# One step of a gated linear recurrence: where the value products of a 128-row block are written

## The chip, the core and the metric

The kernel runs on one core of a Trainium2 chip. TensorE (PE in the profile) multiplies matrices into PSUM banks, VectorE (DVE) and ScalarE (ACT) read those banks and round or combine, GpSimd (POOL) works on data in SBUF, and SyncE (SP) issues most of the DMAs. Each engine works through its own list of instructions in order; the engines wait for each other by semaphores. The metric is the device time of one execution in microseconds. A run's time is a little longer than the span in its profile, which goes from the first to the last instruction.

## The reference

One layer of a hybrid decoder runs on a prompt of 1024 rows and on 64 rows of 8 sampled sequences, with model width 1024. Both go through a gated feed-forward part (FFN, inner width 2816), a mixer and a second FFN. The mixer projects its input once, and splits the result between sliding-window attention and a gated linear recurrence with four heads of 128 keys and 128 values. The recurrence in the reference, cut to what matters:

```python
def step(S, inp):
    qb, kb, gb, vb = inp
    G = jnp.cumsum(gb, axis=2)
    ...
    A = jnp.einsum('bhtk,bhsk,bhtsk->bhts', qb, kb, decay)
    o = jnp.einsum('bhts,bhsv->bhtv', A, vb) + jnp.einsum('bhtk,bhkv->bhtv', qb * jnp.exp(G), S)
    G_last = G[:, :, -1:, :]
    S = jnp.exp(G_last[:, :, 0, :])[..., None] * S + jnp.einsum(
        'bhsk,bhsv->bhkv', kb * jnp.exp(G_last - G), vb)
    return S, o
...
o = rms_norm(o, hg_out_norm[l]) * jax.nn.silu(hg...)
```

For each chunk of rows there is an output `o`, made from the masked products `A` with the values and from the queries with the old state `S`, and a new state, made from the decayed old one and from keys times values. The output is then normalised per head and multiplied with a gate.

## The kernel before

**Tiling.** The rows are cut into three parts: part 0 has 320 (256 of the prompt and the 64 sampled ones), parts 1 and 2 have 384 each. The recurrence goes in blocks of 128 rows: two in part 0, three in each of the others, eight in all. Every large product is made of three products of rounded halves (`mm3`, L258 to L262), with the weights as `hi` and `lo`: the cast L240 on ACT, the difference L241 on DVE. These are the rows named `mm` in the profile.

**Two kinds of work interleaved.** The large products are written out in order: projections of the first FFN, `w_in` of a part, `w_out` of a part, and so on. The mixer of a part is a Python generator that runs beside them. After every few products the code calls `tick()`, and a tick advances each running stream by its rate (0.88, 1.08 and 1.24 steps for the mixers of parts 0, 1, 2); a step is what a generator does up to its next `yield`. Beside the mixer, streams for the norms run in the same way. Part 0's mixer runs beside the last products of the first FFN, part 1's beside `w_out` of part 0 and `w_in` of part 2, part 2's beside `w_out` of part 1 and the first columns of the second FFN. `need(...)` runs what is left of a stream to its end.

**Inside the mixer.** `mixer(n)` takes steps in turns from two chains (`both`): the recurrence (`intra`, then one `hgrn_block` per block) and the attention (`attn_block` per block, in part 0 also the sampled rows). `intra` builds the masked products `At` and the decayed queries `Q` and keys `K` of the whole part. A `hgrn_block` then goes in these steps:

- keys: four transposes `kT` (L1446) into a PSUM bank, copied to `kn` by ACT (L1448). In the first block of a part one empty step follows (L1450 to L1451).
- values: `av`, the products of `At` with the values (L1454) and, except in the very first block, of `Q` with the state `st` (L1457).
- state: `u`, the products of `kn` with the values (L1461), then the update of `st` by DVE (L1463 or L1466). In the same step `finish_hgrn` begins: squares of `av` by ACT (L1400), the mean (L1401) and the root (`rsqrt`, L212 to L229) on DVE, and the scaling of `av` by it (L1403).
- two empty steps, then the transposes `hT` (L1409), the gate (L1411) and the rounding into the input of `w_out` (`put_mix`, L1196 and L1197).

**Buffers.** PSUM has eight banks: four for the large products (tag `mm`) and four (tag `ax`) that `kT`, `av`, `u`, `hT`, the attention's `sc`, `pT`, `pv`, `pvT`, `oT`, the transposes `tr` and the means `rb` share. `av` holds its bank from its first product to L1403, `u` to the update of the state.

**Order.** The kernel's context has a planner: `TileContext(nc, schedule_with_timeline_sim=True)`. It takes the order in which the code is written as priority and makes each engine's list with timings of its own model; an instruction that its model holds not ready lets later ones pass. So the written place of an instruction is a priority and not a position: in the trace the squares L1400 stand ahead of `u` in several blocks, though they are written behind it. Where buffers of a tag are all taken, an instruction that needs one waits in that plan.

Of the kernel before, what the change touches and what calls it, by code (L numbers as in the profile page):

```python
# [47 lines left out]
def tile_step(ctx: ExitStack, tc: tile.TileContext, A: dict, O: list):  # L48
# [17 lines left out]
    def axbank(s="ax"):  # L66
        return ps.tile([P, 512], F32, tag="ax", bufs=4, name=uid(s))
# [1011 lines left out]
    def mixing(tp, h):  # L1079
        w_in, w_out = A["w_in"], A["w_out"][0]  # L1080

        def t2(shape=(P, 512)):
            return tmp2("t2", shape)
# [311 lines left out]
        def finish_hgrn(n, bank, r, c0):  # L1395
            sm = small()
            o = t2((P, 4, P))
            b4 = bank.rearrange("p (a t) -> p a t", a=4)
            for a in range(4):
                S.activation(o[:r, a], b4[:r, a], AF.Square, accum_out=sm[:r, 0, a:a + 1])  # L1400
            V.tensor_scalar(sm[:r, 0, :4], sm[:r, 0, :4], 1.0 / P, EPS, op0=ALU.mult, op1=ALU.add)  # L1401
            rsqrt(sm[:r, 1, :4], sm[:r, 0, :4], (sm[:r, 2, :4], sm[:r, 3, :4]))
            V.tensor_tensor(o[:r], b4[:r], sm[:r, 1, :4].unsqueeze(2).to_broadcast([r, 4, P]), op=ALU.mult)  # L1403
            yield
            yield
            yield
            tb = axbank("hT").rearrange("p (a t) -> p a t", a=4)
            for a in range(4):
                PE.transpose(tb[:, a, :r], o[:r, a], ident[:r, :r])  # L1409
            m = t2((P, 4, P))  # L1410
            V.tensor_tensor(m[:, :, :r], tb[:, :, :r], Z[n]["g"][:, :, c0:c0 + r], op=ALU.mult)  # L1411
            put_mix(n, 1, slice(c0, c0 + r), m[:, :, :r])
            yield
# [21 lines left out]
        def hgrn_block(n, b):  # L1435
            z = Z[n]
            c0 = b * P
            first = state[0] is None
            if first:
                state[0] = tp.tile([P, 4, P], F32, tag="st", name="st")  # L1440
            st = state[0]
            At, Q, K, D = [M[n][i] for i in ("At", "Q", "K", "D")]
            cs = slice(c0, c0 + P)
            tb = axbank("kT").rearrange("p (a t) -> p a t", a=4)
            for a in range(4):
                PE.transpose(tb[:, a], K[:, a, cs], ident)  # L1446
            kn = t2((P, 4, P))
            S.copy(kn, tb)  # L1448
            yield
            if b == 0:  # L1450
                yield  # L1451
            ob = axbank("av")
            for a in range(4):
                PE.matmul(ob[:, a * P:(a + 1) * P], At[:, b, a], z["v"][:, b, a * P:(a + 1) * P],  # L1454
                          start=True, stop=first)
                if not first:
                    PE.matmul(ob[:, a * P:(a + 1) * P], Q[:, a, cs], st[:, a], start=False, stop=True)  # L1457
            yield
            ub = axbank("u").rearrange("p (a t) -> p a t", a=4)
            for a in range(4):  # L1460
                PE.matmul(ub[:, a], kn[:, a], z["v"][:, b, a * P:(a + 1) * P], start=True, stop=True)  # L1461
            if first:
                V.tensor_copy(st, ub)  # L1463
            else:
                for a in range(4):
                    V.scalar_tensor_tensor(st[:, a], st[:, a], D[:, a, b:b + 1], ub[:, a],  # L1466
                                           op0=ALU.mult, op1=ALU.add)
            yield from finish_hgrn(n, ob, P, c0)
# [156 lines left out]
        def mixer(n):  # L1625
            MT[n] = new_h(n)
            at = [attn_block(n, b) for b in range(NPB[n])]
            M[n] = {}
            hg = [intra(n, M[n])] + [hgrn_block(n, b) for b in range(NPB[n])]
            if n == 0:  # L1630
                at = at + [sample_attn(), kv_out(0)]
                hg = hg + [sample_hgrn()]
            if n == 2:
                at.append(kv_out(2))
            yield from both(chain(*hg), chain(*at))
            if n == 2:
                nc.sync.dma_start(O[4][0, 0].rearrange("h k v -> k h v"), state[0])
# [277 lines left out]
```

## Time and profile before

| what | value |
|---|---|
| median of 3 runs | 1936.35 us (1936.21 to 1937.49) |
| profiled execution, its own time | 1939.13 us |
| its span, first to last instruction | 1937.4 us |
| TensorE busy | 1923.1 us, 99% of the span |
| VectorE, ScalarE, GpSimd busy | 1430.7, 946.0 and 186.1 us |
| granted TensorE clock, mean | 0.999 |
| DMA | 375.56 MB, mean 194 GB/s |

A row of a timeline has the start in us from the span's start, the length in us, the engine, the line of the code, the operation, the tiles written and read, the shape, and how many instructions of that kind follow each other; in brackets stands how long the engine was idle before it, and who ended that. Matmuls are pipelined, so the next one starts before the last one's row ends: the distance of two starts is what a matmul takes of TensorE's time. One of these products in 32-bit floats goes as two instructions, so four products of 128 columns are "x8". A row of the waits has who waited, for whom, the sum in us, the number of times and the longest. The mixers of the three parts lie between about 690 and 1320 us.

### The profile page before, as it was taken

What the parts mean: (1) busy time and instruction counts of PE and PEld (TensorE: products, weight loads), DVE (VectorE), ACT (ScalarE), POOL (GpSimd) and SP (SyncE); (2) the same over time, 40 slices, a digit from 0 to 9 for tenths busy, and PEclk for the clock granted to TensorE, in tenths of its full rate; (3) what the DMA queues carried; (4) which work ended last, traced back from release to release, by engine and by line L of the source; (5) the groups of instructions that cost most, each with busy time, mean ns of one, the idle gap of its engine ahead of it and who ended that gap; (6) DMA issues with size and microseconds to landing.
All of it is one profiled execution on the core that took longest, in us unless ns stands there. A gap on an engine that the chain in (4) does not pass through costs nothing.

```text
span 1937.4 us, 34843 instructions
## 1 busy us (share of the span) xinstructions
PE 1923.1 (99%) x13547; PEld 1806.1 (93%) x13547; DVE 1430.7 (74%) x2469; ACT 946.0 (49%) x1701; POOL 186.1 (10%) x227
## 2 busy tenths in 40 slices
PE   9999999999999999999999999999999999999998
PEld 9999999999998987788999888989999999999886
DVE  6896789877568666787678758756987887656666
ACT  5553444444455434545445545846544444445452
POOL 0300000000004022020221212000000000000102
PEclk9999999999999999999999999999999999999999
DMA  6643676555767556765334344546555555667974
GB/s 248 209 133 115 232 267 247 206 191 184 242 217 242 180 155 215 283 220 163 114 102 153 99 140 142 164 147 209 185 198 192 198 188 189 210 228 241 308 255 141
DMA packets 175750, 375.56 MB, mean 194 GB/s; under 512 B 16144, under 2 KB 67536, under 8 KB 175568
## 3 DMA queue, kind: packets, MB, share of 16 engines
q1 hardware_dynamic: 169680, 362.84, 56.0%
q10 hardware_dynamic: 5904, 10.49, 1.5%
q8 instruction: 106, 1.74, 0.4%
q14 instruction: 60, 0.49, 0.1%
HBM read 290.86 MB, written 83.39 MB: 193 GB/s over the span
## 4 chain that ended last, share of the span: by engine, by line
PE 88%; DMA 6%; DVE 3%; ACT 1%; issue 1%; POOL 1%; SPq 0%; ACTq 0%; DVEq 0%; POOLq 0%
PE mm L260 27%; PE mm L262 26%; PE mm L261 26%; DMA ar<-fa 1%; DMA xt<-in_x_rest_dram 1%; DMA ar<-act 1%; PE lv L1337 1%; PE sc L1237 1%; DMA raw<-in_ffn_w_gu_dram 1%; PE pv L1283 1%; DVE w L241 1%; PE pT L1269 1%; PE c L262 0%; PE c L260 0%; PE c L261 0%
## 5 line engine op out<-in xcount | busy, mean ns | idle before, releaser
L260 PE MATMUL mm<-h,wsph 128*128 128x320 f32 (+1 forms) x1344 | 427.2, 319 | 0.4 <-DVE big L814 0.4
L261 PE MATMUL mm<-h,wsph 128*128 128x320 f32 (+1 forms) x1344 | 425.5, 317 | 0.2 <-DVE h L241 0.2
L262 PE MATMUL mm<-h,wspl 128*128 128x320 f32 (+1 forms) x1344 | 422.6, 316 | 0.0
L241 DVE TENSOR_TENSOR wspl<-raw,wsph 128x1024 fp32r<-128x1024 f32 x208 | 260.8, 1255 | 125.2 <-ACT wsph L240 124.1
L240 ACT CAST wsph<-raw 128x1024 fp32r<-128x1024 f32 x208 | 217.8, 1049 | 254.0 <-PE mm L261 199.3
L260 PEld LDWEIGHTS mm<-h,wsph 128*128 128x128 f32 x1344 | 252.2, 188 | 4.2 <-issue 2.3
L261 PEld LDWEIGHTS mm<-h,wsph 128*128 128x128 f32 x1344 | 252.5, 188 | 3.9 <-issue 2.3
L262 PEld LDWEIGHTS mm<-h,wspl 128*128 128x128 f32 x1344 | 251.9, 188 | 3.4 <-issue 3.1
L240 ACT CAST w<-raw 128x512 fp32r<-128x512 f32 (+1 forms) x208 | 153.8, 745 | 199.9 <-PE mm L261 96.2
L261 PE MATMUL mm<-h,w 128*128 128x384 f32 (+1 forms) x736 | 245.6, 334 | 0.3 <-DVE h L622 0.3
L260 PE MATMUL mm<-h,w 128*128 128x384 f32 (+1 forms) x736 | 245.7, 334 | 0.2 <-ACT h L620 0.2
L262 PE MATMUL mm<-h,w 128*128 128x384 f32 (+1 forms) x736 | 239.6, 333 | 0.5 <-POOL w L613 0.4
L241 DVE TENSOR_TENSOR w<-raw,w 128x512 fp32r<-128x512 f32 (+1 forms) x208 | 178.3, 861 | 72.6 <-ACT w L240 71.7
L261 PE MATMUL mm<-w,h 128*128 128x512 f32 x462 | 180.5, 391 | 0.7 <-DVE w L241 0.7
L260 PE MATMUL mm<-w,h 128*128 128x512 f32 x462 | 180.8, 394 | 0.0
L262 PE MATMUL mm<-w,h 128*128 128x512 f32 x462 | 179.8, 391 | 0.0
L260 PE MATMUL mm<-big,w 128*128 128x384 f32 x528 | 176.7, 335 | 0.3 <-ACT big L806 0.2
L261 PE MATMUL mm<-big,w 128*128 128x384 f32 x528 | 176.5, 334 | 0.0
L262 PE MATMUL mm<-big,w 128*128 128x384 f32 x528 | 176.0, 334 | 0.0
L261 PEld LDWEIGHTS mm<-h,w 128*128 128x128 f32 x736 | 138.1, 188 | 1.1 <-DVE h L622 0.8
L260 PEld LDWEIGHTS mm<-h,w 128*128 128x128 f32 x736 | 138.1, 188 | 0.8 <-ACT h L620 0.5
L262 PEld LDWEIGHTS mm<-h,w 128*128 128x128 f32 x736 | 137.6, 188 | 1.0 <-POOL w L613 0.7
(367 smaller groups left out, 3353.8 us busy)
## 6 DMA issues: line engine op xcount, KB each, us to landing
raw<-in_ffn_w_gu_dram SPq DMA_DIRECT2D x162, 512.0 KB
raw<-in_ffn_w_down_dram SPq DMA_DIRECT2D x74, 512.0 KB
raw<-in_w_in_dram SPq DMA_DIRECT2D x54, 512.0 KB
ar<-fa SPq DMA_DIRECT2D x70, 384.0 KB
big<-in_ffn_w_down_dram SPq DMA_DIRECT2D x88, 256.0 KB
fb<-big SPq DMA_DIRECT2D x44, 512.0 KB
fa<-big SPq DMA_DIRECT2D x22, 768.0 KB
raw<-fb SPq DMA_DIRECT2D x30, 512.0 KB
```

The lines of the kernel that those rows point to most:

```text
L240: made['S'] = S.copy(hi, src).ins
L241: (lo_eng or V).tensor_tensor(lo, src, hi.bitcast(F32), op=ALU.subtract)
L260: PE.matmul(out, a[0], b[0], start=first, stop=False, skip_group_check=resume)
L261: PE.matmul(out, a[0], b[1], start=False, stop=False, skip_group_check=resume)
L262: return PE.matmul(out, a[1], b[0], start=False, stop=last, skip_group_check=resume).ins
L1237: PE.matmul(banks[g][rows(hq), i, cs], zq[rows(g), 2 * pr + i, b * P + 64 * hq:b * P + 64 * hq + 64], kx[rows(g), k0 + cs.start:k0 + cs.st ...
L1269: PE.transpose(tb2[hq][:, g, i, slot], pt[g][rows(hq), c:c + P], ident[rows(hq), rows(hq)])
L1283: PE.matmul(ob[par][rows(g), :, hq], vn[rows(par), b + (blk + hq) // 2, rows(g)], pT[hq][rows(par), g, :, PLACE[hq][blk]], start=alone or ...
L1337: PE.matmul(b5[32 * i:32 * i + 32, b, a], K[:, a, cs], Q[:, a, cs], start=True, stop=True)
```

## The change

In `hgrn_block` the `yield` between the value products and the state products goes, and a `yield` is added behind the copy of the keys. The number of steps of a block is the same. The keys are transposed and copied in one step as before; then there is an empty step (two in a part's first block); then `av` and `u` are written in one step, `av` first, and `finish_hgrn` begins in it as before.

```diff
             kn = t2((P, 4, P))
             S.copy(kn, tb)
             yield
+            yield
             if b == 0:
                 yield
             ob = axbank("av")
...
                           start=True, stop=first)
                 if not first:
                     PE.matmul(ob[:, a * P:(a + 1) * P], Q[:, a, cs], st[:, a], start=False, stop=True)
-            yield
             ub = axbank("u").rearrange("p (a t) -> p a t", a=4)
             for a in range(4):
                 PE.matmul(ub[:, a], kn[:, a], z["v"][:, b, a * P:(a + 1) * P], start=True, stop=True)
```

## The prediction

> **What bounds the kernel.** I read the page's busy times first, then the stretches of the span, then TensorE's own waits, and last the timelines around the eight recurrence blocks.
>
> ```profile
> span 1937.4 us, 34843 instructions
> PE 1923.1 (99%) x13547; PEld 1806.1 (93%) x13547; DVE 1430.7 (74%) x2469; ACT 946.0 (49%) x1701; POOL 186.1 (10%) x227
> 690.00:960.00 270.00, 267.39 (x2328) 227.51 (x2327) 193.32 (x405) 125.27 (x249) 55.57 (x61) 1.00 0.60 193
> 960.00:1150.00 190.00, 190.00 (x1981) 175.67 (x1980) 139.69 (x282) 95.93 (x200) 41.88 (x60) 1.00 0.41 127
> 1150.00:1320.00 170.00, 169.27 (x1672) 151.63 (x1671) 116.19 (x255) 103.39 (x220) 18.52 (x32) 1.00 0.47 148
> ```
>
> The last three rows are the stretches of the mixer: length, then busy time of PE, PEld, DVE, ACT and POOL, then the granted clock. The reader is to see that TensorE hardly ever stands: 2.6, 0.0 and 0.7 us in the three. What stands there is listed whole in its waits between 690 and 1320 us:
>
> ```profile
> PE spT L1517 <- ACT t L1512: 1.3, 1, 1.3
> PE av L1454 <- ACT t L1292: 1.1, 1, 1.1
> PE pv L1283 <- DVE t L1274: 0.5, 2, 0.4
> PE kT L1446 <- POOL big L1388: 0.4, 1, 0.4
> ```
>
> So 1.3 + 1.1 + 0.5 + 0.4 = 3.3 us is all that better order could win back in the mixer. A loss has no such lid: whatever makes TensorE wait is added to the time.
>
> **The change part by part.** It removes no instruction, adds none, and issues no DMA elsewhere; nothing passes a DMA of SP's queue or work of POOL's. In each block the value products `av` (L1454, L1457) are written one step later, right ahead of the state products `u` (L1461). The number of steps stays, so `u`, the state update and all attention steps keep their places.
>
> First: how many blocks does that reach? In four of the eight, `av` and `u` already run back to back, because `av` had to wait: the second block of part 0 (its `av` is the wait of 1.1 us above) and the three of part 2. Here is the last of part 2, on TensorE:
>
> ```profile
> 1243.30 0.38 PE L1454 MATMUL av<-big,big 128*128 128x128 f32 x2
> 1245.08 1.06 PE L1461 MATMUL u<-big,t 128*128 128x128 f32 x8
> 1189.09 1.06 PE L1461 MATMUL u<-big,t 128*128 128x128 f32 x8
> 1189.91 0.39 PE L260 MATMUL mm<-h,wsph 128*128 128x320 f32 x1
> 1190.14 0.31 PE L261 MATMUL mm<-h,wsph 128*128 128x320 f32 x1
> 1190.28 0.31 PE L262 MATMUL mm<-h,wspl 128*128 128x320 f32 x1
> ```
>
> `av` takes 1245.08 - 1243.30 = 1.78 us when `u` follows; `u` takes 0.82 (from the first block of part 2, third and fourth row), and the first projection behind it is 0.23 long where 0.14 is usual, 0.09 for the change of shape. Together 2.69 us. In the other four (the first block of part 0, all of part 1) projections lie between. The first `u` of part 1, and its second block:
>
> ```profile
> 1004.35 1.05 PE L1461 MATMUL u<-big,t 128*128 128x128 f32 x8
> 1029.82 0.38 PE L1454 MATMUL av<-big,big 128*128 128x128 f32 x2
> 1031.38 0.39 PE L1457 MATMUL av<-st,big 128*128 128x128 f32 x2
> 1031.52 0.42 PE L260 MATMUL mm<-h,wsph 128*128 128x384 f32 x1
> 1031.78 0.34 PE L261 MATMUL mm<-h,wsph 128*128 128x384 f32 x1
> 1035.76 1.05 PE L1461 MATMUL u<-big,t 128*128 128x128 f32 x8
> 1036.57 0.42 PE L260 MATMUL mm<-h,wsph 128*128 128x384 f32 x1
> 1036.83 0.34 PE L261 MATMUL mm<-h,wsph 128*128 128x384 f32 x1
> 1037.00 0.34 PE L262 MATMUL mm<-h,wspl 128*128 128x384 f32 x1
> ```
>
> Apart, `av` costs 1031.52 - 1029.82 = 1.70, `u` 0.81, and each is followed by a projection of 0.26 where 0.17 is usual: 1.70 + 0.81 + 2 x 0.09 = 2.69 us. Joined or apart is the same 2.69. Term for TensorE: 4 x 0.0 = 0.0 us.
>
> Second: what follows `av`. The squares on ACT (L1400), nine small steps (L1401 and the eight of the root) and the scaling L1403 on DVE, then the transposes `hT` (L1409) on TensorE. Counts and sizes stay; they are now due 6 us later, and the question is whether `hT` then finds its input. The tightest is the third block of part 1; its rows on ACT, DVE and TensorE:
>
> ```profile
> 1060.78 0.39 PE L1457 MATMUL av<-st,big 128*128 128x128 f32 x2
> 1061.20 0.28 ACT L1400 ACTIVATE t<-av 128x128 f32<-128x128 f32 x1 [0.54 <-PE av L1457]
> 1065.16 1.05 PE L1461 MATMUL u<-big,t 128*128 128x128 f32 x8
> 1066.30 1.28 ACT L1157 ACT_TABLE_LOAD   x1
> 1067.59 1.49 ACT L1157 ACTIVATE big<-big 128x1536 f32<-128x1536 f32 x1
> 1068.99 1.16 ACT L240 CAST h<-ht 128x320 fp32r<-128x320 f32 x3
> 1070.19 0.60 PE L1211 MATMUL oT<-ident,t 128*128 128x128 f32 x4
> 1072.97 0.69 DVE L1403 TENSOR_TENSOR t<-av,sm 128x512 f32<-128x512 f32 x1
> 1074.71 0.68 DVE L1197 TENSOR_TENSOR h<-oT,h 128x512 fp32r<-128x512 f32 x1
> 1074.83 0.89 PE L1237 MATMUL sc<-kx,big 64*64 64x192 f32 x16
> 1079.86 0.60 PE L1409 MATMUL hT<-ident,t 128*128 128x128 f32 x4
> ```
>
> `av` ended at 1060.78 + 0.39 = 1061.17 and L1403 started 11.8 us behind that. Put `av` where `u` starts, 1065.16; with 1.78 + 0.17 of its tail it ends at 1067.11, L1403 by the same distance starts at 1078.91 and ends at 1079.60, 0.26 us ahead of `hT`. No wait, but only just. The same sum in the block quoted above it: `av` ends 1037.71 in place of 1031.77, its L1403 and `hT` are
>
> ```profile
> 1037.24 0.69 DVE L1403 TENSOR_TENSOR t<-av,sm 128x512 f32<-128x512 f32 x1
> 1048.98 0.60 PE L1409 MATMUL hT<-ident,t 128*128 128x128 f32 x4
> ```
>
> and L1403 would end at 1037.24 + 5.94 + 0.69 = 1043.87, 5.1 us early. So for this term I take 0.0 us. Upper end, at the third block: ACT works in order, and the squares may come to stand behind the table load, the sigmoid and the casts, which end at 1070.15 in place of 1067.11. That is 3.04 us more; L1403 ends at 1082.64 and `hT` waits 2.78 us. I take the lower value, for the kept distance of 11.8 us is already the longest seen (5.5 us in the block before), so it holds DVE work that need not follow the squares.
>
> [...]
>
> Third: `u` now starts 1.78 us later, the update L1466 with it. The next reader of the state is the following block's `av`, no sooner than 1029.82 against the first `u` of part 1 at 1004.35: covered by over 20 us, 0.0.
>
> Fourth: PSUM. `av`, `u`, `oT`, `sc` and the mean of the norms share four banks. At 1074.83 `sc` needs two: `u`'s was free, and `av`'s came free at 1073.66, behind L1403. With L1403 late it takes `oT`'s, free at 1074.71 + 0.68 = 1075.39, 0.56 us later than now. Between 0 and 0.6; I take 0.0, since the planner has projections to put ahead of `sc`, and without these it costs the 0.6.
>
> Fifth: the wait of 1.1 us at `av` in part 0. Its block keeps its order, so 0.0; lower end -1.1.
>
> Sum: 0.0 + 0.0 + 0.0 + 0.0 + 0.0 on the profiled execution's 1939.13 us (span 1937.4 and 1.7 around it). The median of the runs shown is 1936.35, 2.8 us below that execution; the forecast against it is 1936.3.
>
> **The rivals.** (a) The later `av` of part 0 no longer meets the copy L1292: its 1.1 us go, 1935.2. For it: one step later, the copy is 1.1 us nearer its end. Against it: this `av` already runs behind its written place. If every wait of the mixer went, it would be 3.3 us, 1933.0.
>
> (b) `hT` is late in the third block of part 1: 1936.35 + 2.78 = 1939.1. For it: a margin of 0.26 us only. Against it: TensorE has projections at hand that the planner can put first.
>
> (c) Slower: vector and scalar work for the weights is held up behind the moved chain, in all three blocks of part 1. DVE and ACT take their work in order. If the planner places L1401 where it would have come on its own count and `av` is 5.94 us later, DVE stands up to that long, and the rounding of the next weights (L241) behind it. The cover is the weights that are ready ahead:
>
> ```profile
> ACT wsph L240 <- PE mm L261: 34.7, 19, 4.0
> ```
>
> In 960 to 1150 us the casts waited 19 times, up to 4.0 us, for TensorE to give a buffer back, so weights are about one tile of 24 products ahead, 24 x 0.17 = 4.1 us. From a stand of 4.1 us on it decides; at 5.94 us each block pays 1.8, three 5.5 us: 1941.9. Against it: the planner's order is made anew, with `av` in its new place, and in part 1 TensorE waited 0.0 us under the order that it made before.
>
> (d) The change does nothing: the planner draws `av` ahead again wherever TensorE has room. Same time as the forecast, 1936.3, but the rows of `av` would not move.
>
> **How the numbers follow.** No measurable change by the forecast 0.46, (d) 0.06, (a) 0.08, (b) 0.10: all within 0.2%, which is 3.9 us and about what a measurement of this kernel can tell from no change; together 0.70. (c) 0.24, slower by over 0.2%. Faster by over 0.2% needs more than the 3.3 us of waits in the mixer, so 0.06 for an order that also trims what I cannot see. The range goes down to 1933.0, all waits gone, and up to 1941.9, the whole of (c); beyond it I leave about 0.15. The likeliest case alone is 1935.2 to 1939.1.
>
> **What would show it.** In the trace after, each `u` of part 1 follows its `av` without a projection between, with 1.78 + 0.82 us; the four blocks that already ran so keep their order; TensorE stays at about 190.0 us busy of 190 in part 1; `hT` of the third block of part 1 waits under 1 us. (b) would show as a wait of `hT` for L1403, (c) as waits of projections for L241. The prediction is wrong if TensorE's waits in the mixer rise by 4 us or more, or if waits appear in stretches that the change doesn't touch, since the planner's order there was made anew as well.

## The result, and the profile after

The changed kernel takes 1942.53 us (median of 10 runs, 1941.56 to 1945.70) against 1937.82 us (median of 10, 1936.21 to 1939.19) of the kernel before, measured beside it: a ratio of 1.0026, with a 95% interval of 1.0018 to 1.0034. It is slower by 4.7 us, a little more than the 0.2% that a measurement can tell. I had forecast no change.

The top of the page after, and behind it the three stretches of the mixers (length, busy time of PE, PEld, DVE, ACT, POOL, clock, DMA):

```profile
span 1941.7 us, 34833 instructions
PE 1927.2 (99%) x13547; PEld 1808.4 (93%) x13547; DVE 1430.3 (74%) x2469; ACT 946.4 (49%) x1701; POOL 190.3 (10%) x227
```

```profile
690.00:960.00 270.00, 268.04 (x2331) 228.10 (x2331) 196.50 (x405) 125.55 (x250) 56.00 (x61) 1.00 0.60 193
960.00:1150.00 190.00, 190.00 (x1975) 174.84 (x1974) 138.53 (x280) 95.74 (x200) 42.64 (x60) 1.00 0.40 127
1150.00:1320.00 170.00, 168.79 (x1648) 149.40 (x1646) 113.80 (x246) 100.47 (x215) 19.45 (x32) 1.00 0.46 145
```

TensorE has the same 13547 instructions and the same clock, but is busy for 1927.2 us in place of 1923.1: the span grew by 4.3 us and the busy time by 4.1. In the mixers it stands 2.0 + 0.0 + 1.2 = 3.2 us, against 3.3 before. So in sum no wait was added. Of its waits in the mixers, that of `av` is 0.5 us shorter and that of `pv` 0.3 us longer; those of `spT`, 1.3, and `kT`, 0.4, are as before. The two that changed:

```profile
PE pv L1283 <- DVE t L1274: 0.8, 1, 0.8
PE av L1455 <- ACT t L1292: 0.6, 1, 0.6
```

Where does the busy time come from? The groups of TensorE's instructions between 690 and 1330 us show it, three groups of before and then the same three of after (count, busy time, mean ns of one, idle time before):

```profile
L1237 PE MATMUL sc<-kx,big 64*64 64x192 f32 (+1 forms) x256 | 15.6, 323 | 0.0
L1283 PE MATMUL pv<-t,vn 64*64 64x128 f32 x360 | 13.7, 278 | 0.5 <-DVE t L1274 0.5
L1269 PE MATMUL pT<-ident,t 64*128 64x64 f32 x240 | 12.8, 231 | 0.0
```

```profile
L1237 PE MATMUL sc<-kx,big 64*64 64x192 f32 (+1 forms) x256 | 16.5, 323 | 0.0
L1283 PE MATMUL pv<-t,vn 64*64 64x128 f32 x360 | 14.8, 279 | 0.8 <-DVE t L1274 0.8
L1269 PE MATMUL pT<-ident,t 64*128 64x64 f32 x240 | 14.0, 233 | 0.0
```

As many products, each as long as before (the mean of one is the same within 2 ns), and yet 0.9 + 1.1 + 1.2 = 3.2 us more of TensorE. These are the attention's three kinds of products on 64-row tiles (`64*64` and `64*128` where the projections have `128*128`), and the change touches none of them. By these sizes two or four such tiles fit where a projection takes 128*128, and products on different tiles ran at the same time: in the rows below, four of `sc` start within 0.1 us. Before, they did so more often. I call the products of one kind that follow each other on TensorE a visit. The third block of part 1 is the clearest place. Before, `sc` was one visit of 16 instructions, 1074.83 to 1075.65. After, on TensorE and DVE:

```profile
1074.80 0.87 PE L1237 MATMUL sc<-kx,big 64*64 64x192 f32 x8
1075.60 0.50 PE L260 MATMUL mm<-wsph,h 128*128 128x512 f32 x1
1075.93 0.40 PE L261 MATMUL mm<-wspl,h 128*128 128x512 f32 x1
1076.17 0.39 PE L262 MATMUL mm<-wsph,h 128*128 128x512 f32 x1
1077.41 0.87 PE L1237 MATMUL sc<-kx,big 64*64 64x192 f32 x8
1078.20 0.50 PE L261 MATMUL mm<-wspl,h 128*128 128x512 f32 x1
1075.53 0.68 DVE L1403 TENSOR_TENSOR t<-av,sm 128x512 f32<-128x512 f32 x1
```

Eight instructions take 1075.60 - 1074.80 = 0.80 us, and the other eight 0.79; all sixteen together took 0.82. `sc` writes two PSUM banks, and in the code each takes the products of one half of the array's rows (`banks[g]` those of `rows(g)`; `pT` and `pv` divide their banks likewise). How many of its instructions start within the first 0.1 us of the visit tells the two cases apart, before and then after:

```profile
1074.82:1074.92 0.10, 0.09 (x4) 0.09 (x8) 1.00 0.00 0
```

```profile
1074.79:1074.89 0.10, 0.09 (x2) 0.09 (x4) 1.00 0.00 0
```

Four at once with both banks, two at once with one. So a visit with one bank did half the work in the same time, 0.80 us against 0.82; I take the other half of the array to be empty then. (VectorE's L1247 reads two results at 1076.73 and 1077.00, ahead of the second visit at 1077.41, which fits one whole bank in each visit; the trace doesn't name the banks.) Why one bank: `av` now ends 4.1 us later (about 1065.3 in place of 1061.2), L1403 starts at 1075.53 in place of 1072.97, and L1197, which reads `oT`, stands behind it on DVE (at 1076.13 in place of 1074.71). At 1074.80 neither of their banks was free (L1403 ended at 1076.21, L1197 at 1076.81), and the planner put what it could, the half of `sc` whose bank was there. The price is 0.80 + 0.79 - 0.82 = 0.77 us, and 0.19 for one more change of shape there and back (1075.93 - 1075.60 = 0.33 where 0.24 follows, and some 0.1 on the product ahead): 1.0.

The second place is the second block of part 2, and there it is the transposes `pT` and the products `pv`. Before:

```profile
1228.83 1.01 PE L1269 MATMUL pT<-ident,t 64*128 64x64 f32 x16
1229.77 0.42 PE L260 MATMUL mm<-h,wsph 128*128 128x320 f32 x1
1232.49 0.90 PE L1283 MATMUL pv<-t,vn 64*64 64x128 f32 x24
1233.32 0.66 PE L1409 MATMUL hT<-ident,t 128*128 128x128 f32 x4
```

And after, with the row that follows each visit (a third single `pT`, 1229.25 to 1229.45, is left out):

```profile
1227.86 0.28 PE L1269 MATMUL pT<-ident,t 64*128 64x64 f32 x1
1228.07 0.41 PE L262 MATMUL mm<-h,wspl 128*128 128x320 f32 x1
1228.41 0.27 PE L1269 MATMUL pT<-ident,t 64*128 64x64 f32 x1
1228.61 0.42 PE L260 MATMUL mm<-h,wsph 128*128 128x320 f32 x1
...
1230.09 0.52 PE L1269 MATMUL pT<-ident,t 64*128 64x64 f32 x5
1230.54 0.42 PE L260 MATMUL mm<-h,wsph 128*128 128x320 f32 x1
1232.21 0.71 PE L1269 MATMUL pT<-ident,t 64*128 64x64 f32 x8
1232.85 0.55 PE L513 MATMUL tr<-ident,big 128*128 128x128 f32 x3
1233.90 0.65 PE L1283 MATMUL pv<-t,vn 64*64 64x128 f32 x8
1234.49 0.41 PE L262 MATMUL mm<-h,wspl 128*128 128x320 f32 x1
1235.72 0.87 PE L1283 MATMUL pv<-t,vn 64*64 64x128 f32 x16
1236.52 0.41 PE L260 MATMUL mm<-h,wsph 128*128 128x320 f32 x1
```

`pT` took 1229.77 - 1228.83 = 0.94 in one visit, and takes 0.21 + 0.20 + 0.20 + 0.45 + 0.64 = 1.70 in five. (Its 0.94 was not the best it can do: the visit of 16 at 961.73, shown with e14 below, takes 0.64. So in this block the kernel before had lost part of the overlap already.) `pv` took 0.83 and takes 0.59 + 0.80 = 1.39. That is 1.3 us, and five more changes of shape at 0.19 would be 1.0 (an estimate from the first place). In this block the change had swapped two things on ScalarE. The copy of the transposes `tr` (L518), which frees their PSUM bank, before and then after, beside the first exponential of the probabilities (L1255):

```profile
1225.03 0.46 ACT L1255 ACTIVATE t<-t,sm 128x192 f32<-128x192 f32 x1
1226.89 0.56 ACT L518 ACTIVATE big<-tr,cols 128x384 f32<-128x384 f32 x1
```

```profile
1224.56 0.58 ACT L518 ACTIVATE big<-tr,cols 128x384 f32<-128x384 f32 x1
1226.45 0.46 ACT L1255 ACTIVATE t<-t,sm 128x192 f32<-128x192 f32 x1
```

Before, `tr` and `av` lay between each other on TensorE, with three of `tr` even between `av` and `u`, and the copy came last. The end of it, before:

```profile
1224.33 0.39 PE L1457 MATMUL av<-st,big 128*128 128x128 f32 x2
1224.55 0.49 PE L513 MATMUL tr<-ident,big 128*128 128x128 f32 x3
1224.88 1.06 PE L1461 MATMUL u<-big,t 128*128 128x128 f32 x8
```

After, `av` is written later, `tr` goes first (its last before `av` at 1224.25), and its bank is free before the exponentials are done, which themselves begin 1.4 us later. My reading is that a bank for `pT` is there too soon, so that the plan places the transposes of this one bank singly, as it expects their inputs. The trace fits that in part: the first eight go one behind another and VectorE copies them at 1230.65, before the other eight begin at 1232.21. But the last exponential has ended at 1228.31, while the third single transpose goes at 1229.25 and the five at 1230.09, so it is the list that spaces them and not a wait. What the runs separate here is said with e6.

The third place is the third block of part 2, before and then after:

```profile
1273.66 0.89 PE L1283 MATMUL pv<-t,vn 64*64 64x128 f32 x24 [0.36 <-DVE t L1274]
```

```profile
1277.19 0.66 PE L1283 MATMUL pv<-t,vn 64*64 64x128 f32 x12 [0.85 <-DVE t L1274]
1277.78 0.44 PE L1301 MATMUL pvT<-ident,t 128*128 128x128 f32 x2
1278.15 0.65 PE L1283 MATMUL pv<-t,vn 64*64 64x128 f32 x12
```

Here `pv` is cut in two (0.59 and about as much again, in place of one visit of some 0.82) and its wait is 0.5 us longer. This cut is not one between the halves: four of the first twelve start within the first 0.1 us, as many as before, so both halves work in each visit, but each for a part of it alone.

To put a size on every place, the traces are aligned by work: from the distance of each two starts on TensorE the usual distance for that shape is taken, and what is left is added up. The difference to before in the three places (by the times of before), with the sum of the three groups above, for every run that follows:

```
run    1020-1080  1215-1245  1262-1300   sc+pv+pT, us    ratio [95%]
before     -          -          -         42.1            -
after    +1.4       +2.3       +0.9        45.3 (+3.2)   1.0026 [1.0018, 1.0034]
e1        0.0       +2.3       +0.9        44.2 (+2.1)   1.0015 [1.0006, 1.0023]
e2       +1.3        0.0        0.0        43.2 (+1.1)   1.0009 [1.0000, 1.0018]
e3       +1.4       +6.1       +0.9        43.9 (+1.8)   1.0034 [1.0021, 1.0047]
e4       +0.8       +6.4        0.0        41.7 (-0.4)   1.0021 [1.0012, 1.0029]
e5       +0.4       +2.3       +0.9        44.4 (+2.3)   1.0017 [1.0009, 1.0026]
e6        0.0       +0.5       +0.9        42.9 (+0.8)   1.0011 [1.0002, 1.0019]
e7       +0.3       -0.3        0.0        42.1 ( 0.0)   1.0003 [0.9994, 1.0012]
e8       +0.8        0.0        0.0        41.8 (-0.3)   0.9996 [0.9987, 1.0005]
e9       +0.3       +0.5       +0.9        43.2 (+1.1)   1.0006 [0.9998, 1.0015]
e10      +0.8       +2.3       -0.4        42.6 (+0.5)   1.0006 [0.9997, 1.0015]
e11      +0.3       +1.1       -0.4        41.2 (-0.9)   1.0000 [0.9991, 1.0009]
e12       0.0       +1.3       -0.8        40.6 (-1.5)   0.9995 [0.9986, 1.0004]
e13      +0.1       +0.5       -0.4        42.2 (+0.1)   0.9995 [0.9985, 1.0005]
e14      +0.5        0.0       +0.6        45.4 (+3.3)   1.0013 [1.0003, 1.0022]
```

For after, 1.4 + 2.3 + 0.9 = 4.6 us of the 4.7 measured. Ahead of 845 us, single profiled executions differ by up to 2.4 us, so a place is read more exactly than a whole span. For the kernels whose edits reach many blocks (e4, e8 and e10 to e14) the three places are not the whole: they also lose and gain elsewhere.

### The profile page after: what moved, and what is told of

Read it like the earlier page. It is cut to its first block, busy times and chain, and to the rows that moved or that the text cites. A ratio compares the mean times of both kernels' runs of the same rounds, so it can differ in the third digit from the quotient of the medians.

```text
span 1941.7 us, 34833 instructions
## 1 busy us (share of the span) xinstructions
PE 1927.2 (99%) x13547; PEld 1808.4 (93%) x13547; DVE 1430.3 (74%) x2469; ACT 946.4 (49%) x1701; POOL 190.3 (10%) x227
## 4 chain that ended last, share of the span: by engine, by line
PE 92%; DMA 3%; DVE 3%; issue 1%; ACT 1%; POOL 0%; SPq 0%; ACTq 0%; DVEq 0%; POOLq 0%
PE mm L260 28%; PE mm L261 28%; PE mm L262 28%; DMA ar<-act 1%; DMA ar<-fa 1%; PE lv L1337 1%; PE sc L1237 1%; PE pv L1283 1%; PE pT L1269 1%; DMA xt<-in_x_rest_dram 1%; PE c L262 0%; PE c L260 0%; PE c L261 0%; DMA raw<-in_ffn_w_gu_dram 0%; DMA big<-in_ffn_w_gu_dram 0%
## 5 line engine op out<-in xcount | busy, mean ns | idle before, releaser
L241 DVE TENSOR_TENSOR wspl<-raw,wsph 128x1024 fp32r<-128x1024 f32 x208 | 261.6, 1259 | 123.4 <-ACT wsph L240 122.1
L241 DVE TENSOR_TENSOR w<-raw,w 128x512 fp32r<-128x512 f32 (+1 forms) x208 | 176.7, 854 | 74.7 <-ACT w L240 73.8
```

The source lines that it names most:

```text
L241: (lo_eng or V).tensor_tensor(lo, src, hi.bitcast(F32), op=ALU.subtract)
```

## The experiments

**Where it is lost (e1, e2).** e1 has the change in the second block of part 2 alone, e2 in parts 0 and 1 alone.

```diff
-            yield
+            joined = n == 2 and b == 1      # e2: n < 2
+            if joined:
+                yield
 ...
+            if not joined:
+                yield
             ub = axbank("u").rearrange("p (a t) -> p a t", a=4)
```

> The change in the second block of part 2 alone, the other seven blocks as before. Theory A (shape changes): the loss is in TensorE's order around this block, where the planner now breaks the attention's transposes pT (L1269), the products pv and the transposes tr into pieces with projections between; each change of shape costs 0.1 to 0.3 us, and no wait is needed. A expects 3 us or more of the 4.7 us lost: ratio to before 1.0015 to 1.0026. Theory B (each moved block pays its share by chains that end later): an eighth of the loss or, as this block's av already ran next to u, nothing: 0.9995 to 1.0006.

> The change in parts 0 and 1 (five blocks), part 2 as before. Theory A: these are the blocks where av really moves, but the pieces on TensorE are not broken there; at most 1.3 us, what part 1 lost in the two traces: 0.9997 to 1.0007. Theory B (each moved block pays): nearly all of the loss: 1.0018 to 1.0026.

e1 measured 1.0015, e2 1.0009, together 1.0024 of the 1.0026. By the medians that is 2.5 us, a little under the 3 that theory A asked for, and 1.3, about the most that it allowed; theory B, an equal share for each moved block, fits neither. In e1 part 1 is as before and both places of part 2 are lost; in e2 it is the other way round. So the third place follows from the change in the second block of part 2, though it lies a block later; why, I did not test by itself.

**Keeping `pT` together (e3, e4, e8).** In e3 the changed kernel issues the 16 transposes of the second block of part 2 behind the one that is ready last. e4 does this everywhere in the kernel before, e8 everywhere but in that block.

```diff
-                for i in range(2):
-                    for g in range(2):
+                lead = None
+                for i in (1, 0):
+                    for g in (1, 0):
 ...
-                                    PE.transpose(...)
+                                    with tc.issue_after(lead) if lead is not None else nullcontext():
+                                        tp_ = PE.transpose(...)
+                                    lead = tp_.ins if lead is None else lead
```

> The whole change, and in the second block of part 2 the sixteen transposes pT of each pair are held together: the one that is ready last is written first, and the others are issued behind it. Nothing else is forced. Theory A: the pieces of pT at 1227.9 to 1232.9 us go, with some 1.5 us of the loss, and what the planner built on them: 1939 to 1941 against 1942.5, ratio to before 1.0004 to 1.0018. Theory B: pT's order is a symptom; ratio stays at 1.0022 to 1.0030.

> The kernel before, with the transposes pT held together in all blocks of the attention in the same way. Theory A: the planned order of TensorE changes between projections and other work fewer times (397 stretches instead of 412), 15 x 0.1 to 0.3 us less: 1.5 to 4 us faster, ratio 0.9979 to 0.9993, unless the one that is waited for makes TensorE stand. Theory B: 0.9997 to 1.0010.

> The kernel before, with the transposes pT held together in all blocks but the second of part 2, where holding them made TensorE stand 3.7 us and the clock fall. Theory A: 401 stretches instead of 412, 11 x 0.1 to 0.3 us less: ratio 0.9982 to 0.9995. If changes of shape are not what costs: 0.9997 to 1.0010.

e3 and e4 were slower, at 1.0034 and 1.0021. Some of the pieces were gone: e4 spends 0.4 us less than before in the three groups. In e3 `pT` goes in two visits of 8 in that block, but `pv` still in 8 and 16. And a wait came that neither kernel has, 3.4 us in e3 and 3.7 in e4. That of e4, and its window behind it:

```profile
PE tr L513 <- DVE sm L1247: 3.7, 1, 3.7
```

```profile
1220.00:1224.00 4.00, 3.34 (x13) 3.34 (x14) 2.62 (x13) 3.95 (x7) 0.00 (x0) 0.50 0.41 131
```

A stand of 3.7 us, and behind it a granted clock of 0.50 for four us: together most of the +6.4 of the table. So these two runs decide nothing on the pieces. e8 leaves that block out and has no such wait. It came to 0.9996 [0.9987, 1.0005], short of the 0.9982 to 0.9995 expected: what it saves in `pT` (12.8 to 11.7 us) it loses for the larger part in `sc` (15.6 to 16.4). In the third block of part 1 its `sc` is one visit of 16, with no projection between and no wait in the trace, and yet it takes twice as long as before:

```profile
1074.70 1.70 PE L1237 MATMUL sc<-kx,big 64*64 64x192 f32 x16
```

The scaling of `av` ends at 1075.39 in e8, in the middle of this visit. That fits a second bank that comes free only then, but no run tests it.

**Giving the bank back early (e5).** The changed kernel, and in the third block of part 1 ScalarE copies `av` out of PSUM at once; squares and scaling read the copy.

```diff
+            early = (n == 1 and c0 == 256)
+            if early:
+                S.copy(o[:r], b4[:r])
 ...
-            V.tensor_tensor(o[:r], b4[:r], ...)
+            V.tensor_tensor(o[:r], o[:r] if early else b4[:r], ...)
```

> The whole change, and in the third block of part 1 alone ACT copies av out of its PSUM bank right away (one more copy of 128x512, 0.6 us of ACT), squares and scaling then read the copy. Theory A (banks split visits): with the bank free early the attention's products sc of this block are one visit of sixteen again, not two of eight. In the stretch from the block's keys to its last transposes (1050 to 1105 us) TensorE gets back the 1.3 us that the changed kernels lost there; the whole run 1941.0 to 1942.0 against 1942.5, ratio to before about 1.0015 to 1.0022. Theory C (the chain from av through the root to hT is what is late): the copy makes that chain longer, so nothing comes back in that stretch, 1942.5 to 1943.5.

`sc` is whole again and 1050 to 1080 us shows 0.0 in place of +1.0; the group has 15.6 us as before.

```profile
1072.19 0.88 PE L1237 MATMUL sc<-kx,big 64*64 64x192 f32 x16
```

The joined step is still there, with its `av` and `u` side by side. So in that block it was the bank held by the late `av` that cost 1.0 us, and not the joined step. The whole came to 1.0017.

**Putting the copy of `tr` back behind the exponentials (e6).** On top of e1, each copy of `tr` by ScalarE goes behind the last exponential written so far:

```diff
-                    S.activation(a[:, k], bank[:, :384], AF.Copy, scale=g)
+                    with tc.issue_after(made['exp']) if 'exp' in made else nullcontext():
+                        S.activation(a[:, k], bank[:, :384], AF.Copy, scale=g)
 ...
-                        S.activation(pt[g][...], pt[g][...], AF.Exp, ...)
+                        made['exp'] = S.activation(pt[g][...], pt[g][...], AF.Exp, ...).ins
```

> The change in the second block of part 2 alone, as in the run of one block, and the ACT copies of the norm's transposes tr (L518) are issued behind the last exponential written so far, as they came to stand in the kernel before. Theory A: the bank of tr then comes free later, pT doesn't begin with one bank and single pieces; the 2.3 us lost at this block fall to 1.5 us or less: 1938.5 to 1940 against 1940.7. If the order of these two on ACT is no part of the cause: 1940 to 1941.5.

The place fell from +2.3 to +0.5, with `pT` in two visits of 8 (the first is shown) and `pv` in one of 24, at 1231.67:

```profile
1227.52 0.71 PE L1270 MATMUL pT<-ident,t 64*128 64x64 f32 x8
```

So the order of these two on ScalarE is a cause of this place. Through what, e6 doesn't separate: with the order, the bank of `tr` comes later and the exponentials come sooner. And e10 below, which copies every `av` out at once, has `pT` in two visits of 8 here as well (at 1226.25 and 1228.11), though its copy of `tr` (1222.63) stands ahead of the first exponential (1224.51); it loses 2.3 us there in another way, with `pv` in two visits of 12 and 0.8 us of waits. So the bank that the late `av` holds may have its part in the five pieces too. The third place stayed at +0.9 in e6, so the copy does not cause that one.

**Joining at the other end (e7).** `av` stays in its old step and `u` with the state update is drawn up to it; the free step comes behind the update.

```diff
                     PE.matmul(ob[:, a * P:(a + 1) * P], Q[:, a, cs], st[:, a], start=False, stop=True)
-            yield
             ub = axbank("u").rearrange("p (a t) -> p a t", a=4)
 ...
+            yield
             yield from finish_hgrn(n, ob, P, c0)
```

> The other way to have values and state in one step: u and the update of the state move up to av's place, av stays, and the free step comes behind them. Theory A: av's bank is asked for when it was in the kernel before and stretches on TensorE stay at 412: ratio 0.9990 to 1.0008, no loss. Theory D (joining the two is what costs, wherever it stands): as slow as the change, 1.0018 to 1.0030.

1.0003 [0.9994, 1.0012], and the three groups have 15.6, 13.7 and 12.8 us, as before. One step for values and update is free; doing the values late is what costs.

**The sum (e9).** The whole change with the edits of e5 and e6 together.

> The whole change, with two things done to it: in the third block of part 1 av is copied out of PSUM by ScalarE at once (as in e5), and the copies of tr's bank at line 518 are issued behind the last exponential (as in e6). If the loss is the sum of three places (+1.4 in part 1, +2.3 in the second block of part 2, +0.9 in the third block of part 2), this takes away 1.0 of the first and 1.8 of the second and leaves 0.4 + 0.5 + 0.9 = 1.8 us: 1937.8 + 1.8 = 1939.6 us, ratio 1.0009. Rival: the places are not independent and the loss only moves (the time stays at 1942.5, ratio 1.0025).

1939.44 us against 1938.04, 1.0006 [0.9998, 1.0015], and 1939.6 was expected. With both causes taken away 0.3 + 0.5 + 0.9 = 1.7 us are left by the table, 1.4 by the medians. So the two add up, within what these runs can tell.

**Is it the number of changes? (e10, e11, e12).** e10 is the changed kernel with e5's copy in every block, e11 the kernel before with it, e12 joins as e7 does, with the copy and e8's order of `pT`. I call a run of products of one kind in TensorE's list a stretch.

> The whole change, and av is copied out of PSUM by ScalarE at once in every block, so that its bank comes free before the normalisation. The planned order of TensorE then has 410 stretches of one shape, against 412 of the kernel before and 424 of the changed one. If the loss is the number of those stretches (4.7 us for 12 more, about 0.4 us each), the time is that of the kernel before: 1937.0 us (ratio 0.9996), within 1936 to 1938.5. Rival: the joined step itself costs the time wherever the banks come free: 1942.5 (ratio 1.0025). Second rival: the added copies on ScalarE make later work late, which shows as waits of TensorE on ScalarE of more than 1 us that the kernel before doesn't have.

> The kernel before, with av copied out of PSUM at once in every block: 403 stretches against 412. By the price of 0.4 us for a stretch: 1937.8 - 9 x 0.4 = 1934.2 us (ratio 0.9981). Rival: only a stretch that a whole bank's wait has split costs what the change showed, others cost 0.1 us: 1937 (ratio 0.9995). Second rival: the copies on ScalarE cost more than they bring: over 1938.5.

> The joined step at the place where av stood (as in e7), av copied out of PSUM at once in every block, and the transposes of the probabilities issued together except in the second block of part 2 (as in e8): 393 stretches against 412. By 0.4 us for a stretch 1937.8 - 19 x 0.4 = 1930.2 us (ratio 0.9961). Rival, after e8, where 11 fewer stretches brought nothing that could be measured: no gain, 1937 us (ratio 0.9995); then the price of a stretch isn't one number, and what was saved stands again as waits for the later start.

All three fell short. e10 lost 1.3 us though it has two stretches fewer than the kernel before; e11 with 9 fewer gained nothing (1.0000), e12 with 19 fewer 0.7 us (0.9995 [0.9986, 1.0004]). So 0.4 us for each stretch was no price at all, only 4.7 divided by 12. The three groups say why in part: in e11 and e12 they fell by 0.9 and 1.5 us, not by the 3.6 and 7.6 that 9 and 19 stretches at 0.4 would be. And what they saved stood again elsewhere: in 1215 to 1245 us these two lost 1.1 and 1.3. No version beat the kernel before by more than its interval.

**Or the halves of the array? (e13, e14).** The kernel before, but inside a visit the tiles of one bank are written behind those of the other, not by turns: e13 for `sc`, e14 for `pT`. The edit of e14:

```diff
-                for i in range(2):
-                    for g in range(2):
-                        for slot, at in ((0, (0, 64)), (1, (128, -64))):
-                            for hq in halves:
+                for hq in halves:
+                    for i in range(2):
+                        for g in range(2):
+                            for slot, at in ((0, (0, 64)), (1, (128, -64))):
```

> The kernel before, with the products of sc written one PSUM bank after the other, in place of by turns. The plan keeps 13 visits of sc with both banks and 6 with one, and has 408 stretches against 412. Theory of the halves: sc x16 has taken 0.82 us because tiles of both banks start within 0.02 us of each other; one bank after the other the visit takes 0.82 + 0.65 = 1.47 us, 13 x 0.65 = 8.4 us more, less at most 4 x 0.4 = 1.6 us for the stretches: 1938.0 + 8.4 = 1946.4 us, at least 1944.8 (ratio 1.0035 to 1.0043). Theory of the number of changes: 0 to 1.6 us less than before, 1936.4 to 1938 us, and sc x16 stays at 0.82.

> The kernel before, with the transposes pT written one PSUM bank after the other, in place of by turns. The plan keeps every visit of pT (9 with all 16 of them) and splits one visit of pv more: 414 stretches against 412. Theory of the halves: a visit of 16 in pairs takes 0.64 us, one bank after the other 16 x 0.0625 + 0.15 = 1.15 us; 9 x 0.5 = 4.5 us, and about 1 for the split pv: 1943.5 us (ratio 1.0028). Theory of the number of changes: 2 x 0.4 = 0.8 us more, 1938.8 us (ratio 1.0004).

e14 is slower, 1.0013 [1.0003, 1.0022], 3.0 us by the medians where the number of changes would give 0.8 and the halves 5.5. `pT` has 15.6 us in place of 12.8. One of its visits in e14, the group of `pT` there, and the same visit before:

```profile
961.96 1.01 PE L1269 MATMUL pT<-ident,t 64*128 64x64 f32 x16
```

```profile
L1269 PE MATMUL pT<-ident,t 64*128 64x64 f32 x240 | 15.6, 233 | 0.0
```

```profile
961.73 0.71 PE L1269 MATMUL pT<-ident,t 64*128 64x64 f32 x16
```

From 0.71 to 1.01. Eight visits of 16 go up by 0.3 each, 2.4 us; the visits of 12 add the rest (the ninth of 16, that of 1228.83, had 1.01 in the kernel before already). These are the same instructions in as many visits of `pT`, and how far the two halves overlap is what has changed; the one `pv` more that is split (13.7 to 14.2 us) makes up the rest of the 3.0. e13 missed: 0.9995, `sc` still takes 0.82 us. Its row, and how many instructions start in its first 0.1 us:

```profile
1074.53 0.89 PE L1237 MATMUL sc<-kx,big 64*64 64x192 f32 x16
```

```profile
1074.52:1074.62 0.10, 0.09 (x4) 0.09 (x8) 1.00 0.00 0
```

Four at once again, though the second bank's products are written eight instructions later. If the list keeps that order, TensorE itself started tiles of the other half ahead of their turn here, where they stood right behind: fully for the eight of `sc` (0.82 us as before), partly for the eight of `pT`, whose visit takes 0.94 us from its first start to the next product's, where sixteen one by one would take 1.15 (the estimate in the expectation; its 0.0625 us for one fits the visits of five and eight above, (0.64 - 0.45) / 3 = 0.063). This doesn't save the changed kernel. There projections on the whole array stand between the two halves, and the rows with x8 show 0.80 and 0.79.

## Why the prediction was wrong

- **"A loss has no such lid: whatever makes TensorE wait is added to the time."** This is where it went wrong first. I looked for losses in waits alone, and the test that I wrote down (waits up by 4 us or more) would have passed: they went from 3.3 to 3.2 us. Most of the loss, 4.1 of 4.3 us of span, is TensorE's own busy time.
- **First, `av` and `u` joined or apart cost 2.69 us.** In part 1 right: `av` starts at 1063.35, `u` at 1065.13, 1.78 apart, with no projection between, and e7 shows that joining is free. But that "the four blocks that already ran so keep their order" fell in the second block of part 2. It had been misread: there `av` and `u` did not run back to back before, `tr` lay between and among them (the rows of 1224.33 to 1224.88). The term of 4 x 0.0 looked at the moved products and not at their neighbours: +2.3 us there, +0.9 a block later.
- **Second, the chain to `hT`: 0.0, and held.** L1403 of the third block of part 1 starts at 1075.53 (I had 1078.91) and `hT` at 1080.83 without a wait. So rival (b) did not happen. The margin was larger than I had it: `av` does not take the place of `u`, it goes ahead of it, and ends at 1065.30 in place of the forecast 1067.11.
- **Third, the state: 0.0, and held**, though `u` did not even start later there: 1065.13 against 1065.16.
- **Fourth, PSUM: "between 0 and 0.6; I take 0.0".** The right place and the right mechanism, the bank that the late `av` holds, but the term is +1.0 us there, above my upper end. I let the planner's projections hide a late bank. They do hide the wait, and by going between the two halves they part them. Here the cover itself was the cost. e5 shows that the bank was the cause. Another 0.4 us of part 1, between 1020 and 1050, is a visit of `pT` cut into 4 and 12.
- **Fifth, the wait of `av` in part 0.** It went from 1.1 to 0.6 us; a gain of 0.5, inside the bounds.
- **(a)** gave those 0.5. **(c)** ends at 1941.9, near the measured time, but by a mechanism that did not happen: TensorE waited 0.0 us in part 1, and no row of L241 stands in its waits there. **(d)** did not happen, since `av` moved.

The sum that would have been right is 1.4 + 2.3 + 0.9 = 4.6 us. The 1.0 of `sc` was within reach of the fourth term: the kernel before has a `sc` in two visits of 8 at 967.75 and 969.14, with rows of 0.82 and 0.87, about as long each as the one of 16 (0.89). The other 3.6 depended on how the plan falls out in neighbouring visits, which I could at most have bounded. Why the third place follows stays open.

## What to carry to other kernels

Where small tiles of two PSUM banks share the array, a bank that comes late can cost without any wait, as in the third block of part 1: the plan filled the gap with other work, and each half then ran alone, 0.80 and 0.79 us, in the time that both had taken together, 0.82. One that comes too soon may do the same, as the second place suggests. So when a change holds a bank longer, look for who takes the next two banks, and compare in the trace the number, the size and the length of its visits (x16 against x8 and x8, or, as in e8, 0.89 against 1.70 at the same x16), since neither the waits (3.3 us before, 3.2 after) nor the mean time of an instruction (323 ns of `sc` in both) showed it. A busy engine is not one that does as much as it could: compare the busy time of a group at equal count (15.6 and 16.5 us for the 256 of `sc`).

## What the runs showed of the hardware

- `sc` took 0.82 us for sixteen instructions with both banks (1074.83 before) and 0.80 for eight with one (1074.80 after); `pT` took 0.64 us for sixteen (961.73 before) and 0.64 for eight (1232.21 after).
- In e13 four instructions of `sc` started in the first 0.1 us, as in the kernel before, though the second bank's are written eight instructions later. That the sixteen stand in the list bank by bank follows from the written order; the trace doesn't name the bank of each. If they do, these products on the two halves did not start in the order of the list, and the first section's "in order" did not hold for them.
- In e4 TensorE stood 3.7 us, up to 1220.66, and was granted a clock of 0.50 in 1220 to 1224 us and 0.62 in the next 2.5. A stand of 1.3 us at `spT`, near 875 us, which most of these kernels have, was followed by 1.00 in the traces of before, after and most others, but by 0.58 in e8 (and 0.57 in e12 and e13), which cost each of these three profiled executions some 1.3 us (by the alignment used for the table). The row of e8:

```profile
876.00:880.00 4.00, 4.00 (x14) 3.68 (x13) 3.93 (x10) 2.66 (x4) 0.00 (x0) 0.58 0.46 130
```

Why the clock behind the same stand was lower in some executions and not in others is open.
